# A list-scheduled hybrid block on one core: the durations in the planner's table are replaced, and a change of GpSimd's code gets a price

## The chip, the cores and the metric

The kernel runs on one core of a Trainium2 chip. The metric is the device time of one execution in microseconds (us). Five engines of the core work side by side, each through its own instructions in order: TensorE (PE, matrix products), VectorE (DVE), ScalarE (ACT), GpSimd (POOL) and SyncE (SP, which issues transfers). Semaphores order the engines among each other.

## The reference

The reference is a network of two layers on 272 tokens (16 learned ones ahead of 256) of width 1024, all in fp32. Cut to what matters:

```python
for i in range(2):
    hn = rms_norm(h, norm_mix_g[i])
    rq, rk, rv, rg, hq, hf, hi, hg, dq, dk, dv, mg = split(hn @ w_in[i])
    o_ret = rms(retention(rope(rq), rope(rk), rv)) * silu(rg)      # chunks of 128, a state
    o_hg = rms(hgrn2(hq, hf, hi)) * silu(hg)                       # gated linear recurrence
    o_da = rms(diff_attention(rope(dq), rope(dk), dv)) * subln_g   # softmax minus lam * softmax
    y = sum(sigmoid(mg) * (stack(o_ret, o_hg, o_da) @ w_branch[i]))
    h = h + y @ w_out[i]
    u = conv3(rms_norm(h, norm_ffn_g[i]) @ w_ffn_in[i])            # 3 taps along the tokens
    h = h + (silu(u_gate) * u_val) @ w_ffn_out[i]
return rms_norm(h, norm_final_g)
```

## The kernel before, in words

**The work.** The features lie on the partitions and the 272 tokens in the free dimension, so each weight tile of 128x128 is the stationary operand of a product with 272 columns (258 for some). fp32 accuracy comes from a split of both sides in a high and a low float32r part, so each weight tile gives three matmuls: `xh` by `whi` (L915), `xl` by `whi` (L916) and `xh` by `wlo` (L917), into a PSUM tile called `main`. These are the "main" matmuls; everything else that PE does is called a side matmul here.

**The weights.** SP brings in 512 KB chunks of eight tiles (`wraw`, three buffers). ACT copies a chunk to `whi`, DVE subtracts to get `wlo` (`_Weights.next`). This goes on through the whole run and is the largest part of both engines' work.

**The rest.** In each layer a normalisation gives `rstd` (squares summed, `ms` on PE by a matrix of ones, then two ACTIVATEs `rstd` on ACT after a load of ACT's function table). The first four products of a normalisation read the unscaled `h` (split into `xh`, `xl`) and are scaled behind the product; from the fifth on (`DEFER = 4`, `Norm.next`) they read `y = h * rstd`, which POOL forms in eight pieces, ACT rounds to `xh` and DVE completes to `xl`. There are four such normalisations ahead of products: two in each layer, the second one ahead of the conv FFN's input product, called fi here.

- HGRN2: a cumulative product by levels, in which PE adds shifted copies (`lev`, L1107) of what DVE has formed (`hf`, `hq`, `extra`), and then `pm`, `px`, `ho` with the values `vt` and `vm`. The values come through a path of their own: ACT copies them out of PSUM (`vsrc`), POOL takes the halves apart (`apart`), SP transposes by DMA (`turned`), POOL puts them together (`vt`), and copies the last tokens out (`tails`), which PE turns (`vm`).
- Differential attention: scores `ds`, then row sums and a combination of two softmaxes on DVE (`two_a`), turned on PE (`wt`, L1317), made to `wts` on ACT and POOL, then `do` by the values. The heads' outputs are normalised over the partitions with POOL's PARTITION_ALL_REDUCE (`hr<-hsq`).
- The convolution: three taps as ACT's `two_b` and DVE's SCALAR_TENSOR_TENSOR on `two_b`, then `ghi` and `glo`.

**What sets the order.** Nothing is issued as it is written. Every call to an engine goes through `_Engine.__getattr__`, which works out a `cost` from the method and the number `n` of elements to a partition and files an operation with `_Plan.add`, along with a due time `key`. Due times run on a clock that each main matmul triple moves on by its own cost (L905). Then `_Plan.order` walks a planned time line: on each engine it takes, among the operations whose inputs are there in the plan, the one that can start first, and among those the one with the smallest `key`. An input from another engine counts as there `CROSS` = 0.4 us behind its end; PE adds `BACK` = 0.09 us where a main follows a side matmul, a side matmul takes its turn by `key + HOLD` (3.0 us), and nothing but mains may start more than `EARLY` = 12 us ahead of its key. A weight chunk is due `LEAD` = 6 us ahead of its first use. The order found is then issued as it stands, so an error of the plan shows on the chip as an engine that waits for a row which stands too late in another engine's order.

In the planned time line an engine without work is first moved on to the time at which its next operation becomes ready, and the operation is then chosen:

```python
            if op is None:
                engines[e] = t
                continue
```

In the profile all of this is under L607, the one line in which the planned operations are called; the main matmuls, `lev`, `wt` and a few others have lines of their own.

Of the kernel before, what the change touches and what calls it, by code (L numbers as in the profile page):

```python
# [13 lines left out]
F32R = mybir.dt.float32r  # L14
# [11 lines left out]
T = META + SEQ  # L26
# [11 lines left out]
BANK = 512  # L38
# [49 lines left out]
def _ktiles(name):  # L88
    return FK if name == "fo" else KD
# [267 lines left out]
class _Plan:  # L357
# [3 lines left out]
    CROSS = 0.4  # L361
    FREE = 0.5
    SWITCH = 1.3
    SETS = {AF.Exp: "le", AF.Ln: "le", AF.Silu: "silu", AF.Sigmoid: "sigmoid"}

    def __init__(self, tc):
# [87 lines left out]
    def order(self):  # L454

        times, mains = [m.key for m in self.main], set(self.main)
        for op in self.ops:
            i = bisect.bisect_right(times, op.key - EARLY) - 1
            if i >= 0 and op not in mains:
                self.queue(op, self.main[i])  # L460
        left = {}
        for op in self.ops:
            for n in op.tiles:
                left[n] = left.get(n, 0) + 1
        free = {tag: [0.0] * k for tag, k in self.room.items()}
        held, out = set(), []
        engines = {"pe": 0.0, "act": 0.0, "dve": 0.0, "pool": 0.0, "sp": 0.0}
        later = {e: [] for e in engines}
        now = {e: [] for e in engines}
        count = 0  # L470
        tables = "le"
        beside = False

        def push(op):
            nonlocal count
            count += 1
            heapq.heappush(later[op.engine], (op.ready, count, op))

        for op in self.ops:
            if op.need == 0:  # L480
                push(op)

        def start(op, t):

            want = {}
            for n in op.tiles:
                if n not in held:
                    want[self.tag[n]] = want.get(self.tag[n], 0) + 1
            for tag, k in want.items():
# [12 lines left out]
        self.busy = {e: 0.0 for e in engines}  # L502
        todo = len(self.ops)
        while len(out) < todo:
            best = None
            for e, t0 in engines.items():
                while later[e] and later[e][0][0] <= t0:
                    _, c, op = heapq.heappop(later[e])
                    now[e].append((c, op))
                found = None  # L510
                for c, op in now[e]:
                    t = start(op, t0)
                    if t is not None and (found is None or (t, rank(op, t), c) < found[:3]):
                        found = (t, rank(op, t), c, op)
                if later[e]:
                    t1 = later[e][0][0]
                    if found is None or t1 < found[0]:
                        found = (t1, 0.0, -1, None)
                if found is not None and (best is None or found[0] < best[0]):
                    best = found + (e,)  # L520
            if best is None:
                raise RuntimeError("no order: " + str([(e, [o.tiles for _, o in now[e]][:4]) for e in now]))
            t, _, c, op, e = best
# [3 lines that stand above are left out]
            now[e].remove((c, op))  # L527
            cost = op.cost
            if op.func in self.SETS and self.SETS[op.func] != tables:
                tables = self.SETS[op.func]  # L530
                cost += self.SWITCH
                if tables == "le":
                    out.append(None)
                    todo += 1
            for n in op.tiles:
                if n not in held:
                    held.add(n)
                    f = free[self.tag[n]]
                    f.remove(min(f))
            if e == "pe":  # L540
                if op in mains:
                    cost += BACK if beside else 0.0
                beside = op not in mains
            engines[e] = t + cost
            self.busy[e] += cost
            done = t + cost + (2.0 if e == "sp" else 0.0)
            for n in op.tiles:
                left[n] -= 1
                if left[n] == 0:
                    free[self.tag[n]].append(done + self.FREE)  # L550
            for o in op.after:
                o.need -= 1
                if o.engine != e:
                    o.fed = max(o.fed, done + self.CROSS)
                o.ready = max(o.ready, done + (self.CROSS if o.engine != e else 0.0))
                if o.need == 0:
                    push(o)
            if op.run is not None:
                out.append(op)
            else:  # L560
                todo -= 1
        return out
# [11 lines left out]
class _Engine:  # L574
# [5 lines left out]
    def __getattr__(self, method):  # L580
        f = getattr(self.engine, method)

        def call(*args, **kw):
            aps = [(k, x) for k, x in list(enumerate(args)) + list(kw.items()) if isinstance(x, bass.AP)]
            outs = [x for k, x in aps if k in (0, "out", "accum_out")]
            ins = [x for k, x in aps if k not in (0, "out", "accum_out")]
            n = math.prod(outs[0].shape[1:])
            cost = self.fixed + self.each * n
            if self.name == "act":
                cost += 0.093 * (len(aps) - 2) - (0.043 if ins[0].tensor.name in self.plan.psum else 0.0)  # L590
            elif self.name == "pool" and method != "memset":
                cost += 1.6e-3 * n
            if method == "partition_all_reduce":
                cost = 0.4 + 5.4e-3 * n
            if method == "reciprocal":
                cost += 7 * self.each * n
            elif method == "tensor_tensor_scan":
                cost += self.each * n
            elif method == "transpose":
                cost = 0.11  # L600
            elif method == "matmul" and args[1].dtype == F32R:
                cost = max(0.107, n / 2400 + 0.003)
            elif method == "matmul":
                cost = max(0.214 if args[1].shape[-1] > 32 else 0.07, 4 * n / 2400)
            elif method == "dma_start":
                cost = self.fixed + self.each * n * outs[0].shape[0]
            self.plan.add(self.name, lambda: f(*args, **kw), cost, outs, ins, args[2] if method == "activation" else None)  # L607

        return call

# [55 lines left out]

def _trace(ctx, tc, plan, a, depth, probe):
    nc = tc.nc
    act = _Engine(plan, nc.scalar, "act", 0.094, 0.833e-3)
    dve = _Engine(plan, nc.vector, "dve", 0.068, 1.042e-3)  # L670
    pe = _Engine(plan, nc.tensor, "pe", 0.0, 4 / 2400)
    pool = _Engine(plan, nc.gpsimd, "pool", 0.04, 0.85e-3)
    sync = _Engine(plan, nc.sync, "sp", 0.06, 4 / 360e3)
# [218 lines left out]
    def products(xs, name, j, t0=0):  # L892
# [9 lines left out]
        if (name, j) == ("fo", 3):  # L902

            to[j, 1] = main()[:, 1, :]
        cost = 3 * ((T - t0) / 2400 + 0.003)  # L905
        left = dict.fromkeys(to, _ktiles(name))
        for _, i, k, f in tiles:
            hi, lo = (x[:, t0:] for x in xs(k))
# [80 lines left out]
    for li in range(depth):  # L989
# [4 lines left out]
        t0 = T0 if last else 0  # L994
# [389 lines left out]
        def block(name):  # L1384
            if name not in st:
                st[name] = slot4(name)
            return st[name]
# [9 lines left out]
        def final():  # L1397
# [12 lines left out]
            for t in range(2):  # L1410
                for k in range(KD):
                    pe.matmul(accs[t][k // 4][:, k % 4 * P : (k % 4 + 1) * P], h[:, k, tokens(t)], ident, is_transpose=True, start=k % 4 == 0, stop=False)
            cost = 3 * (BANK / 2400 + 0.012)
            groups = [(t, c) for t in range(2) for c in range(2)]
            chunks = {}
            order = [(k, t, c) for k in range(FK - LATE) for t, c in groups]
# [36 lines left out]
        for name, j in ORDER:  # L1453
# [18 lines left out]
            elif name[0] == "*":  # L1472
                plan.key = clock[0] - MARGIN
                n = name[1:]
                if n == "b2":
                    blocks = [st["da0"], st["da1"]]
                else:
                    t = st["rg" if n == "b0" else "hg"]
# [6 lines left out]
            if name in BASE:  # L1485
# [18 lines left out]
                elif name in ("dq", "dk"):  # L1504
                    t = block(f"{name}{j // 2}")
# [12 lines left out]
                elif name in ("hi", "dv"):  # L1518
                    n = name[0] + "v"
# [13 lines left out]
                else:  # L1533
                    t = block(f"{name}{j // 2}")
# [95 lines left out]
```

## Time and profile before

| | us |
|---|---|
| median of 3 runs | 1305.88 |
| the three runs | 1304.24, 1306.25, 1305.88 |
| profiled execution | 1305.7 |
| its span | 1303.9 |
| PE busy | 1285.8 (99%) |
| DVE busy | 986.7 (76%) |
| ACT busy | 786.7 (60%) |
| POOL busy | 270.3 (21%) |

The span is the time from the first to the last instruction; some 1.8 us of the execution's time lie around it. The mean granted clock of PE was 0.998 of full speed. A row of a timeline gives the start in us from the start of the span, the duration in us, the engine, the line, the operation, what it writes and reads, and in square brackets the idle time of that engine ahead of it with what ended it. A group of equal instructions that follow one another is one row with its count behind the x. A row of the waits gives the waiting engine's operation and the one that released it, then the sum in us, the number of times, and the longest.

### The profile page before, as it was taken

The numbers are of one execution on the slowest core, as the hardware profiler recorded it, in microseconds if no ns is written. First come the engines' busy times: TensorE is split into PE (matmuls) and PEld (weight loads), VectorE is DVE, ScalarE is ACT, GpSimd is POOL, SyncE is SP. The second block draws the span as 40 slices with busy tenths as digits, with TensorE's granted clock in tenths as the row PEclk, the third lists the DMA queues.
The fourth block names the chain that finished last, engine by engine and source line by source line (L and its number), as shares of the span: only waits on it lengthen the run. The fifth ranks groups of instructions, "written<-read, shape, count | busy, mean of one in ns | idle before, by whom it ended". The sixth has DMA issues, their size and how long they took to land.

```text
span 1303.9 us, 28637 instructions
## 1 busy us (share of the span) xinstructions
PE 1285.8 (99%) x11678; PEld 1256.7 (96%) x11678; DVE 986.7 (76%) x1589; ACT 786.7 (60%) x1282; POOL 270.3 (21%) x300
## 2 busy tenths in 40 slices
PE   9999999999999999999999999999999999999998
PEld 9999989999999999999999999899999999999986
DVE  7685897798686789886575768877986867898843
ACT  6746444746576567666456474447466765776643
POOL 5021262423422020000030212634223220200000
PEclk9999999999999999999999999999999999999999
DMA  7664665643744545555555646655446446466653
GB/s 272 200 179 147 173 178 155 164 160 125 199 138 157 182 156 178 183 173 183 175 178 185 186 149 185 179 155 168 159 138 199 145 162 198 144 207 196 201 190 112
DMA packets 86868, 225.36 MB, mean 173 GB/s; under 512 B 32976, under 2 KB 33104, under 8 KB 86736
## 3 DMA queue, kind: packets, MB, share of 16 engines
q1 hardware_dynamic: 86448, 223.00, 55.3%
q8 instruction: 92, 1.51, 0.5%
q10 hardware_dynamic: 288, 0.52, 0.1%
q14 instruction: 40, 0.33, 0.1%
HBM read 216.16 MB, written 1.05 MB: 167 GB/s over the span
## 4 chain that ended last, share of the span: by engine, by line
PE 88%; DVE 9%; issue 1%; ACT 1%; DMA 0%; SPq 0%; DVEq 0%; ACTq 0%
PE main L915 26%; PE main L917 26%; PE main L916 25%; DVE wlo L607 2%; PE fo L1430 2%; PE fo L1431 2%; PE fo L1429 2%; DVE two_b L607 1%; DVE two_a L607 1%; PE lev L1107 1%; PE ds L1291 1%; PE ho L607 1%; PE ro L607 1%; PE do L607 1%; DVE two_c L607 1%
## 5 line engine op out<-in xcount | busy, mean ns | idle before, releaser
L915 PE MATMUL main<-xh,whi 128*128 128x272 f32 (+1 forms) x2368 | 682.6, 288 | 0.8 <-ACT whi L607 0.8
L917 PE MATMUL main<-xh,wlo 128*128 128x272 f32 (+1 forms) x2368 | 673.9, 285 | 1.3 <-DVE wlo L607 0.7
L916 PE MATMUL main<-xl,whi 128*128 128x272 f32 (+1 forms) x2368 | 673.3, 284 | 1.5 <-DVE xl L607 1.5
L607 DVE TENSOR_TENSOR wlo<-wraw,whi 128x1024 fp32r<-128x1024 f32 (+1 forms) x411 | 512.0, 1250 | 187.8 <-ACT whi L607 186.6
L607 ACT ACTIVATE whi<-wraw 128x1024 fp32r<-128x1024 f32 (+1 forms) x411 | 427.5, 1042 | 250.9 <-PE main L916 166.3
L917 PEld LDWEIGHTS main<-xh,wlo 128*128 128x128 f32 x2368 | 446.5, 189 | 3.1 <-DVE wlo L607 2.3
L916 PEld LDWEIGHTS main<-xl,whi 128*128 128x128 f32 x2368 | 446.6, 189 | 2.2 <-DVE xl L607 1.9
L915 PEld LDWEIGHTS main<-xh,whi 128*128 128x128 f32 x2368 | 446.7, 189 | 2.0 <-ACT whi L607 1.0
L607 POOL TENSOR_TENSOR y<-h,rstd 128x272 f32<-128x272 f32 x32 | 34.6, 1112 | 318.1 <-ACT rstd L607 318.1
L607 POOL PARTITION_ALL_REDUCE hr<-hsq x36 | 65.8, 1837 | 88.9 <-ACT hsq L607 85.9
L607 DVE SCALAR_TENSOR_TENSOR two_b<-main,small,two_b 128x256 f32<-128x256 f32 (+2 forms) x144 | 65.3, 487 | 24.4 <-ACT two_b L607 22.7
L607 POOL COPY apart<-vsrc 128x512 uint16<-128x512 uint16 x48 | 40.7, 867 | 145.2 <-ACT vsrc L607 145.0
L607 ACT ACTIVATE two_b<-main,small 128x272 f32<-128x272 f32 (+1 forms) x72 | 37.3, 566 | 23.8 <-PE main L917 22.7
L915 PE MATMUL main<-ghi,whi 128*128 128x272 f32 x176 | 51.0, 290 | 0.0
L916 PE MATMUL main<-glo,whi 128*128 128x272 f32 x176 | 50.6, 287 | 0.0
L917 PE MATMUL main<-ghi,wlo 128*128 128x272 f32 x176 | 50.3, 286 | 0.0
L607 POOL COPY vt<-turned 128x512 uint16<-128x512 uint16 x32 | 37.0, 1160 | 29.2 <-DMA turned<-apart 29.0
L915 PE MATMUL main<-b0hi,whi 128*128 128x272 f32 (+1 forms) x128 | 37.9, 296 | 0.0
L915 PE MATMUL main<-b1hi,whi 128*128 128x272 f32 (+1 forms) x128 | 37.8, 296 | 0.0
L915 PE MATMUL main<-yhi,whi 128*128 128x272 f32 (+1 forms) x128 | 36.4, 284 | 0.0
L917 PE MATMUL main<-b0hi,wlo 128*128 128x272 f32 (+1 forms) x128 | 36.4, 284 | 0.0
L917 PE MATMUL main<-yhi,wlo 128*128 128x272 f32 (+1 forms) x128 | 36.3, 284 | 0.0
(235 smaller groups left out, 1970.1 us busy)
## 6 DMA issues: line engine op xcount, KB each, us to landing
wraw<-in_w SPq DMA_DIRECT2D x402, 512.0 KB, 3.4
h<-in_h SPq DMA_DIRECT2D x4, 272.0 KB, 5.1
dec<-in_dec SPq DMA_DIRECT2D x2, 544.0 KB, 4.9
wraw<-in_w SPq DMA_DIRECT2D x4, 256.0 KB, 4.2
const<-in_const SPq DMA_DIRECT2D x1, 937.0 KB, 5.6
turned<-apart SPq DMA_TRANSPOSE x48, 4.0
gain<-in_gl SPq DMA_DIRECT2D x1, 512.0 KB, 5.1
out<-y ACTq DMA_DIRECT2D x2, 256.0 KB, 2.8
```

What stands on the lines that cost most here:

```text
L607: self.plan.add(self.name, lambda: f(*args, **kw), cost, outs, ins, args[2] if method == "activation" else None)
L915: nc.tensor.matmul(o, wh, hi, start=first, stop=False)
L916: nc.tensor.matmul(o, wh, lo, start=False, stop=False)
L917: nc.tensor.matmul(o, wl, hi, start=False, stop=last)
L1107: nc.tensor.matmul(o, keys, x, start=True, stop=True)
L1291: nc.tensor.matmul(ss[m][:, at : at + nk], q[half, hd, q0 : q0 + P], k[half, hd, :nk], start=True, stop=True)
L1429: nc.tensor.matmul(o, gh, wh, start=False, stop=False)
L1430: nc.tensor.matmul(o, gl, wh, start=False, stop=False)
L1431: nc.tensor.matmul(o, gh, wl, start=False, stop=end)
```

## The change

Only the planner's numbers differ; the operations of the program and what they read and write are the same. `_Plan` gets `RELOAD = 8.0`: POOL's `tensor_tensor` and `partition_all_reduce` are filed with their method as their kind, and where the kind differs from the one before, the operation is set 8 us behind the time at which the planned line has POOL, which for an engine that has had no work is the time at which the operation became ready. The formula of `_Engine.__getattr__` is written anew: the fixed part of an ACT operation rises from 0.094 to 0.2 us and of a DVE operation from 0.068 to 0.145 us, POOL's operations get formulas of their own, a transposing DMA 0.7 us more, and a float32r matmul outside of the mains (`ho`, `do`, `lev` and the like) now goes by the general matmul's formula. A main triple costs 0.01 us instead of 0.003 us beyond its columns, three times: 0.370 us instead of 0.349 us for 272 columns.

```diff
+    RELOAD = 8.0
...
-        tables = "le"
+        tables, code = "le", "tensor_tensor"
...
+            if e == "pool" and op.func is not None:
+                if op.func != code:
+                    code, t = op.func, max(t, engines[e] + self.RELOAD)
             engines[e] = t + cost
...
             cost = self.fixed + self.each * n
+            kind = args[2] if method == "activation" else None
             if self.name == "act":
                 cost += 0.093 * (len(aps) - 2) - (0.043 if ins[0].tensor.name in self.plan.psum else 0.0)
-            elif self.name == "pool" and method != "memset":
-                cost += 1.6e-3 * n
-            if method == "partition_all_reduce":
-                cost = 0.4 + 5.4e-3 * n
-            if method == "reciprocal":
+            elif method == "tensor_scalar":
+                cost += 0.065 * (len(aps) - 2) - 0.14
+            elif method in ("scalar_tensor_tensor", "stream_shuffle", "tensor_tensor_reduce"):
+                cost += 0.06
+            elif method == "reciprocal":
                 cost += 7 * self.each * n
-            elif method == "tensor_tensor_scan":
-                cost += self.each * n
+            elif self.name == "pool" and method == "tensor_tensor":
+                cost, kind = 0.55 + 2.1e-3 * n, method
+            elif self.name == "pool" and method == "tensor_copy":
+                cost = 0.35 + 1.0e-3 * n
+            elif method == "partition_all_reduce":
+                cost, kind = 0.2 + 6.3e-3 * n, method
             elif method == "transpose":
                 cost = 0.11
-            elif method == "matmul" and args[1].dtype == F32R:
-                cost = max(0.107, n / 2400 + 0.003)
             elif method == "matmul":
                 cost = max(0.214 if args[1].shape[-1] > 32 else 0.07, 4 * n / 2400)
             elif method == "dma_start":
-                cost = self.fixed + self.each * n * outs[0].shape[0]
+                cost = self.fixed + self.each * n * outs[0].shape[0] + (0.7 if kw.get("transpose") else 0.0)
...
-    act = _Engine(plan, nc.scalar, "act", 0.094, 0.833e-3)
-    dve = _Engine(plan, nc.vector, "dve", 0.068, 1.042e-3)
+    act = _Engine(plan, nc.scalar, "act", 0.2, 0.833e-3)
+    dve = _Engine(plan, nc.vector, "dve", 0.145, 1.052e-3)
...
-        cost = 3 * ((T - t0) / 2400 + 0.003)
+        cost = 3 * ((T - t0) / 2400 + 0.01)
...
-            cost = 3 * (BANK / 2400 + 0.012)
+            cost = 3 * (BANK / 2400 + 0.0133)
```

All five engines' orders change. Three places show how; the lines of the changed kernel are seven higher, and the numbers of the tiles agree.

PE in the second layer's HGRN2, where the tails of the values are turned (`vm`), the keys' and queries' product `pm` is made and a level `lev` begins. Before:

```order
L917 MATMUL main_1321<-xh_14_89,wlo_1327 128x258
L607 MATMUL pm_1299<-qt_1287,kt_1286 128x128
L607 MATMUL vm_1283<-const_79,tails_1269 128x128
L915 MATMUL main_1329<-xh_16_91,whi_1331 128x258
L916 MATMUL main_1329<-xl_17_92,whi_1331 128x258
L917 MATMUL main_1329<-xh_16_91,wlo_1332 128x258
L1107 MATMUL lev_1293<-extra_1290,hf_506_1205 32x32 x32
```

And in the changed kernel:

```order
L924 MATMUL main_1321<-xh_14_89,wlo_1327 128x258
L614 MATMUL vm_1283<-const_79,tails_1269 128x128
L922 MATMUL main_1321<-xh_14_89,whi_1326 128x258
...
L614 MATMUL pm_1299<-qt_1287,kt_1286 128x128
L922 MATMUL main_1321<-xh_14_89,whi_1326 128x258
L923 MATMUL main_1321<-xl_15_90,whi_1326 128x258
L924 MATMUL main_1321<-xh_14_89,wlo_1327 128x258
L1114 MATMUL lev_1293<-extra_1290,hf_506_1205 32x32 x32
```

`vm` moved ahead of `pm`, with six mains between them, and both stand ahead of the last mains of tile 1321; counted in mains, `vm` comes 12 of them sooner.

PE in the first layer's attention, where `do` takes the last tokens' weights `tw`, which DVE forms out of `wt`. Before:

```order
L607 MATMUL wt_602<-const_79,dt_560 128x128
L915 MATMUL main_668<-xh_14_89,whi_673 128x272
L916 MATMUL main_668<-xl_15_90,whi_673 128x272
L917 MATMUL main_668<-xh_14_89,wlo_674 128x272
...
L607 MATMUL do_604<-tw_603,vs_519 128x128
```

And in the changed kernel:

```order
L614 MATMUL wt_602<-const_79,dt_560 128x128
L922 MATMUL main_676<-xh_14_89,whi_681 128x272
L923 MATMUL main_676<-xl_15_90,whi_681 128x272
L924 MATMUL main_676<-xh_14_89,wlo_682 128x272
...
L614 MATMUL do_604<-tw_603,vs_519 128x128
```

Nine mains stood between `wt` and `do` before, 18 stand there now, and the pair has moved back by some 50 rows.

ACT ahead of the first layer's fi, where `rstd` is formed. Before:

```order
L607 ACTIVATE whi_934<-wraw_933 128x1024
L569 ACT_TABLE_LOAD
L607 ACTIVATE rstd_93<-ms_911,eps_84 128x272
L607 ACTIVATE rstd_93<-rstd_93 128x272
L607 ACTIVATE whi_937<-wraw_936 128x1024
L607 ACTIVATE whi_943<-wraw_942 128x1024
L607 ACTIVATE two_b_922<-two_a_921,small_76 128x272 x2
L607 ACTIVATE xh_16_91<-y_950,small_76 128x272 x3
```

And in the changed kernel:

```order
L614 ACTIVATE whi_934<-wraw_933 128x1024
L614 ACTIVATE whi_937<-wraw_936 128x1024
L573 ACT_TABLE_LOAD
L614 ACTIVATE rstd_93<-ms_911,eps_84 128x272
L614 ACTIVATE rstd_93<-rstd_93 128x272
L614 ACTIVATE whi_943<-wraw_942 128x1024
L614 ACTIVATE two_b_922<-two_a_921,small_76 128x272 x2
L614 ACTIVATE whi_946<-wraw_945 128x1024
```

The copy `whi_937` moved ahead of the table load and of `rstd`, and the three `xh` moved behind the next weights (the first of them by eight rows).

More of the change, by code (lines that the diff above doesn't have):

```diff
@@ L605, in call @@
             elif method == "dma_start":
-                cost = self.fixed + self.each * n * outs[0].shape[0]
-            self.plan.add(self.name, lambda: f(*args, **kw), cost, outs, ins, args[2] if method == "activation" else None)
+                cost = self.fixed + self.each * n * outs[0].shape[0] + (0.7 if kw.get("transpose") else 0.0)
+            self.plan.add(self.name, lambda: f(*args, **kw), cost, outs, ins, kind)
         return call
```

## The prediction

> **What bounds the kernel now.** I read the page's busy times first.
>
> ```profile
> span 1303.9 us, 28637 instructions
> PE 1285.8 (99%) x11678; PEld 1256.7 (96%) x11678; DVE 986.7 (76%) x1589; ACT 786.7 (60%) x1282; POOL 270.3 (21%) x300
> ```
>
> PE is busy in 1285.8 of 1303.9 us. The change adds and removes no matmul, so it can reach only the 18.1 us of idle PE, and the first and last few of those belong to loads and to the final transfers. Next I read what PE waits for, from the waits:
>
> ```profile
> PE lev L1107 <- DVE hf L607: 3.2, 2, 1.7
> PE main L916 <- DVE xl L607: 1.5, 2, 1.1
> PE ho L607 <- DVE ho L607: 1.4, 2, 0.8
> PE wt L1317 <- DVE two_a L607: 1.1, 3, 0.5
> PE warm L607 <- POOL eps L607: 1.0, 1, 1.0
> PE main L915 <- ACT whi L607: 0.8, 1, 0.8
> PE main L917 <- DVE wlo L607: 0.7, 3, 0.3
> PE lev L1107 <- DVE tot L607: 0.4, 1, 0.4
> PE lev L1107 <- DVE hq L607: 0.4, 1, 0.4
> PE main L917 <- issue: 0.4, 1, 0.4
> PE do L607 <- DVE tw L607: 0.4, 1, 0.4
> PE lev L1107 <- ACT qt L607: 0.3, 1, 0.3
> PE wt L607 <- DVE wts L607: 0.2, 1, 0.2
> ```
>
> They add up to 11.8 us. The 1.0 behind `eps`, the 0.8 behind `whi` and a part of `wlo` are the program's start; 0.4 is "issue". About 9.3 us are waits for a side engine in the middle, which an order can move: this is all that can be won, 0.7% of the time, and no engine but PE can become the bound as a whole. What can be lost has no such limit: every side result that stands too late in another engine's row adds a wait.
>
> **The change part by part.** I compared the two orders, took each PE row that waits for another engine, and counted how many rows its source and it have moved. Where PE's row moved later and its source did not, the wait goes.
>
> *Attention and the second HGRN2 outputs, a gain.* The two longest of these rows:
>
> ```profile
> 265.90 0.35 PE L607 MATMUL ho<-at,vt 128*128 128x128 f32 x1 [0.81 <-DVE ho L607]
> 323.85 0.49 PE L607 MATMUL do<-tw,vs 128*128 128x128 f32 x2 [0.35 <-DVE tw L607]
> 740.07 0.28 PE L915 MATMUL main<-xh,whi 128*128 128x258 f32 x1
> 740.18 0.28 PE L916 MATMUL main<-xl,whi 128*128 128x258 f32 x1
> ```
>
> A main takes a step of 0.12 us (740.07 to 740.18). `ho` at 265.9 stands 21 mains later in the changed order and its twin of layer 1 some 24, about 2.5 us, while DVE has one `wlo` more ahead of it, 1.2 us: the 1.4 us go. `do<-tw` has nine more mains between it and the `wt` whose result it waits for, 1.1 us against 0.35 us waited, and the `wt` rows move by 9 to 60 mains with their sources ahead. Of 1.1 + 0.4 + 0.2 = 1.7 us I take 1.6. Together -3.0 us. No other work covers this: it was PE's own idle time. The branch's last values come up to 57 rows later; the branch's first product needs them at a row that did not move; PE had no wait there, and I take none.
>
> *The tails of the values, a loss.*
>
> ```profile
> 82.63 0.91 POOL L607 COPY vt<-turned 128x512 uint16<-128x512 uint16 x1 [1.43 <-DMA turned<-apart]
> 83.45 1.24 POOL L607 COPY tails<-vsrc 128x32 f32<-128x32 f32 x1
> 739.55 1.27 POOL L607 COPY tails<-vsrc 128x32 f32<-128x32 f32 x1
> 741.69 0.27 PE L607 MATMUL vm<-const,tails 128*128 128x128 f32 x1
> 741.72 0.37 PE L915 MATMUL main<-xh,whi 128*128 128x258 f32 x1
> 741.92 0.28 PE L916 MATMUL main<-xl,whi 128*128 128x258 f32 x1
> ```
>
> In layer 1 POOL ends `tails` at 739.55 + 1.27 = 740.82, and `vm` ran 0.87 us later. The changed order has `vm` 12 mains sooner, so PE is there at about 740.07 and POOL's row is where it was: 0.75 us lost. In layer 0 `vm` comes 10 mains sooner, and POOL now has `vt`, which waits for a transfer, ahead of the second half of `apart` instead of behind it, so what filled that wait comes after it: 0.3 without the swap's 0.55, 0.8 with it; I take 0.6. Sum +1.35 us, from 0.3 (should the transposes land sooner) to 2.0.
>
> *The norm ahead of fi in layer 0.* ACT's row shows what `rstd` waits for and POOL's when `y` starts:
>
> ```profile
> 471.01 1.28 ACT L569 ACT_TABLE_LOAD   x1
> 473.11 0.49 ACT L607 ACTIVATE rstd<-ms,eps 128x272 f32<-128x272 f32 x1 [0.82 <-PE ms L607]
> 473.97 1.05 ACT L607 ACTIVATE whi<-wraw 128x1024 fp32r<-128x1024 f32 x1
> 474.15 6.60 POOL L607 TENSOR_TENSOR y<-h,rstd 128x272 f32<-128x272 f32 x6 [66.64 <-ACT rstd L607]
> 479.12 3.79 DVE L607 SCALAR_TENSOR_TENSOR two_b<-two_a,small,two_b 128x271 f32<-128x271 f32 x4
> 483.47 0.48 DVE L607 SCALAR_TENSOR_TENSOR xl<-y,small,xh 128x272 fp32r<-128x272 f32 x1
> 483.88 1.21 DVE L607 TENSOR_TENSOR wlo<-wraw,whi 128x1024 fp32r<-128x1024 f32 x1
> 491.17 0.29 PE L916 MATMUL main<-xl,whi 128*128 128x272 f32 x1
> 491.32 1.73 DVE L607 SCALAR_TENSOR_TENSOR two_b<-two_a,small,two_b 128x271 f32<-128x271 f32 x4
> 494.65 0.39 PE L916 MATMUL main<-xl,whi 128*128 128x272 f32 x1 [0.35 <-DVE xl L607]
> ```
>
> [...] The plan, which starts the 8 us at readiness, takes `y` to come 8 us later than it does, and so files `xh` and `xl` late: the first `xl` stands 15 rows later on DVE. Those rows run from 483.88 to the end of the four `two_b` at 493.0, 9.1 us, less three other `xl` of 0.41 each among them, 7.9 us. So `xl` would start at 483.5 + 7.9 = 491.4 and end at 491.9, when PE wants it at 491.17: 0.7 us late. On top, the copy of 1.05 us now stands ahead of the table load of 1.28, and both behind a main just ahead of `ms`: `rstd` ends about 2.1 us later. Eight `y` then lie 2.1 us further into a stretch where DVE never rests, and beside them the four `two_b` took 0.95 us each, against 0.43 at 491.32: about 1.0 us more, so `xl` is 1.7 late. In return the old waits of this stretch, 0.35 here and about as much for two `wlo`, go. Net +0.7 us, from -0.3 (no lateness of `rstd` felt) to +1.7 (nothing given back).
>
> [...]
>
> *The norm ahead of fi in layer 1.*
>
> ```profile
> 1116.89 1.28 ACT L569 ACT_TABLE_LOAD   x1
> 1118.19 0.49 ACT L607 ACTIVATE rstd<-ms,eps 128x272 f32<-128x272 f32 x1
> 1137.25 0.39 PE L916 MATMUL main<-xl,whi 128*128 128x258 f32 x1 [1.15 <-DVE xl L607]
> ```
>
> Here the load ahead of `rstd` drops out of the changed order (31 loads become 29) and `ms` comes three mains later: `rstd` comes 1.28 - 0.37 = 0.9 us sooner, DVE is relieved by about 0.4, and the `xl` for which PE waits 1.15 us is issued ahead of one `wlo`, 1.2 us. But the first `xl`s stand 8 to 14 rows later and a `wlo` takes over part of the wait. I take -0.8, from -1.3 to +1.0.
>
> *What is left.*
>
> ```profile
> 29.16 2.39 POOL L607 TENSOR_TENSOR hq<-hq,rstd 128x544 f32<-128x544 f32 x1
> ```
>
> At the program's start `ms` comes 15 mains later and POOL's `hq` stands ahead of four `y` instead of one; PE waits for none of these `xl` before, so I take +0.2 (0 to 1.2, half of `hq`). In the second HGRN2 half of each layer PE waits for a chain on DVE (`lev` behind `hf`, 3.2 us) whose rows are the same; three mains fewer (layer 0) and three more (layer 1) stand ahead of it, 0.37 each way, 0 in sum. PE goes from mains to side matmuls 140 times instead of 132; a main behind a side matmul takes 0.37 instead of 0.28 us (741.72 against 741.92), so 8 x 0.09 = +0.7. No transfer is among PE's waits, and weights only at the start and at fi, so the new order of SP's rows costs nothing.
>
> Sum: -3.0 + 1.35 + 0.7 - 0.8 + 0.2 + 0 + 0.7 = -0.85 us, from the profiled 1305.7 to 1304.85. That execution lies 0.2 under the median of 1305.88, so I predict 1305.0.
>
> **The rivals.** About 0.2%, 2.6 us, is what a measurement of this kernel can tell from no change: below 1303.3 is faster, above 1308.5 slower.
>
> - *The truer durations hold everywhere.* The same -3.0, and at the norms all `xl` and `wlo` waits outside the start go too (1.5 + 0.6), `vm` finds its tails since the transposes land sooner; the switches remain: -3.0 - 2.1 + 0.7 = -4.4, 1301.5. For it: PE waits in these very rows. Against it: DVE is without a pause at the norms, so an order there moves waits rather than ends them.
> - *The 8 us make the norms late, slower.* The place is the first `xl`s behind `y` in both fi and at the start. If DVE stays at half speed beside `y` longer, or `xh`, which stands behind the next `whi`, holds `xl` up, each fi costs its full lateness with nothing given back: 1.7 + 0.7 (one `xl` more late) for that `xh` in layer 0, 1.7 in layer 1, and half of `hq`'s 2.39 = 1.2 at the start. That replaces my +0.7, -0.8 and +0.2 by 5.3: -0.95 + 5.3 = +4.35, 1310.2. It decides once the lateness over the three norms passes 3.5 us. For it: the first `xl` is already 0.7 late by rows alone. Against it: layer 1's `rstd` comes sooner.
> - *It does nothing:* the rows that moved are not those which PE waits for, within 0.5 us of 1305.9. Against it: `ho` and `do` are exactly such rows.
>
> [...]
>
> **How the numbers follow.** My forecast has 0.52, with a range of its own of 1302.4 to 1307.6 (the bounds of the terms: vm 1.0 down and 0.7 up, norms 1.5 down and 2.8 up, not all at once); of it 0.07 lies below 1303.3 and 0.04 above 1308.5. All-better 0.22, of it 0.20 faster; late norms 0.22, of it 0.20 slower; nothing 0.04. So faster 0.27, same 0.49, slower 0.24. The range runs from 1301.2 to 1309.6, which leaves out half of each outer rival, 2 in 10.
>
> **What would show it.** In the changed profile's PE waits, `ho <- ho`, `do <- tw` and `wt <- two_a` should be gone or under 0.8 us together; a row `vm <- POOL tails` should appear, about 1.35 us in two; `main <- xl` should show one wait of 1 to 2 us near 491 and none near 1137; `y` should still start 0.1 us behind `rstd`, which should end near 476 in layer 0. I am wrong if the waits' sum rises by over 2 us, with `xl` at the norms in front, or if `lev` waits grow: then a chain that I took for unmoved has moved.

## The result: slower by 9.5 us, and the profile after

| | before | after |
|---|---|---|
| median of 6 runs each, us | 1306.07 (1304.24 to 1307.39) | 1315.58 (1314.07 to 1316.07) |
| ratio, 95% interval | | 1.0071 (1.0058 to 1.0084) |
| profiled execution / its span, us | 1305.7 / 1303.9 | 1314.07 / 1312.3 |

The changed kernel is slower by more than the range of the prediction allowed. Its busy times have hardly moved:

```profile
span 1312.3 us, 28618 instructions
PE 1286.3 (98%) x11678; PEld 1257.5 (96%) x11678; DVE 982.7 (75%) x1589; ACT 784.0 (60%) x1280; POOL 277.0 (21%) x300
```

PE is busy for 0.5 us more, in a span longer by 8.4. So the loss is idle time of PE, and the waits name it (the sum, the number of times, the longest):

```profile
PE vm L614 <- POOL tails L614: 6.3, 3, 2.6
PE lev L1114 <- DVE hf L614: 4.6, 3, 2.2
PE main L924 <- DVE wlo L614: 2.9, 5, 1.5
PE main L923 <- DVE xl L614: 2.9, 4, 1.2
PE warm L614 <- POOL eps L614: 1.0, 1, 1.0
PE main L923 <- issue: 0.5, 1, 0.5
PE lev L1114 <- ACT extra L614: 0.5, 1, 0.5
PE main L922 <- ACT whi L614: 0.5, 1, 0.5
PE ho L614 <- DVE ho L614: 0.4, 1, 0.4
PE wt L614 <- DVE wts L614: 0.4, 1, 0.4
```

They add up to 20.0 us against 11.8, 8.2 more. One row that the profile of before lacks altogether makes 6.3 of it. Its three waits are these, PE's rows in its timeline:

```profile
260.52 0.33 PE L614 MATMUL vm<-const,tails 128*128 128x128 f32 x1 [1.25 <-POOL tails L614]
348.29 0.33 PE L614 MATMUL vm<-const,tails 128*128 128x128 f32 x1 [2.59 <-POOL tails L614]
1002.61 0.33 PE L614 MATMUL vm<-const,tails 128*128 128x128 f32 x1 [2.43 <-POOL tails L614]
```

All three are in the attention's values (`dv`), none in HGRN2. Before, PE came to the same three products without a wait, but with little to spare:

```profile
258.89 0.27 PE L607 MATMUL vm<-const,tails 128*128 128x128 f32 x1
344.91 0.27 PE L607 MATMUL vm<-const,tails 128*128 128x128 f32 x1
994.59 0.27 PE L607 MATMUL vm<-const,tails 128*128 128x128 f32 x1
```

Their `tails` ended on POOL at 258.27, 344.22 and 993.47, that is 0.62, 0.69 and 1.12 us ahead. What POOL does ahead of the longest of the three waits stands in its own timeline. Before:

```profile
332.84 1.17 POOL L607 COPY apart<-vsrc 128x512 uint16<-128x512 uint16 x2 [0.76 <-ACT vsrc L607]
333.96 1.35 POOL L607 COPY tails<-vsrc 128x32 f32<-128x32 f32 x2
337.24 1.91 POOL L607 COPY vt<-turned 128x512 uint16<-128x512 uint16 x1 [1.93 <-DMA turned<-apart]
339.06 1.65 POOL L607 COPY apart<-vsrc 128x512 uint16<-128x512 uint16 x1
340.66 1.76 POOL L607 COPY vt<-turned 128x512 uint16<-128x512 uint16 x1
342.34 1.58 POOL L607 COPY apart<-vsrc 128x512 uint16<-128x512 uint16 x1
343.86 0.36 POOL L607 COPY tails<-vsrc 128x32 f32<-128x32 f32 x2
```

After:

```profile
333.47 1.63 POOL L614 COPY apart<-vsrc 128x512 uint16<-128x512 uint16 x2 [0.92 <-ACT vsrc L614]
335.08 1.06 POOL L614 PARTITION_ALL_REDUCE hr<-hsq  x1
336.02 1.02 POOL L614 COPY tails<-vsrc 128x32 f32<-128x32 f32 x2
339.88 0.79 POOL L614 COPY vt<-turned 128x512 uint16<-128x512 uint16 x1 [2.84 <-DMA turned<-apart]
340.58 2.44 POOL L614 COPY da<-tw 128x64 f32<-128x64 f32 x2
342.96 1.83 POOL L614 COPY vt<-turned 128x512 uint16<-128x512 uint16 x1
344.71 3.22 POOL L614 COPY apart<-vsrc 128x512 uint16<-128x512 uint16 x2
347.88 0.36 POOL L614 COPY tails<-vsrc 128x32 f32<-128x32 f32 x2
```

The last two of the `tails` that `vm` needs stand at the end of both. From the first `apart` to their end it takes 343.86 + 0.36 - 332.84 = 11.38 us before and 14.77 after, 3.4 more. The attention's last all-reduce (1.06) and its two `da` copies (2.44), which before stood ahead of the row's start, are in it now and take 3.3 us with their overlaps; the wait for the transposes is 0.9 longer, and the copies proper take 0.8 less. In layer 1 the stretch ahead of 1002.61 is 13.84 us against 10.84, with an all-reduce inside it that stood ahead of it before; its two `da` copies are inside in both, and it waits 0.2 us for transposes against 2.4 before. Near 260 no attention row is inside; the stretch is 12.15 us against 11.56 and starts 1.6 us later, and two `apart` and two `vt` of 1.6 to 1.8 us each stand ahead of the last `tails`. So what the three have in common is the place of the `tails` behind other rows of POOL; a longer wait for a transfer is part of one of them only.

How the time runs apart, from the starts of the same main matmul in both traces: after is 1.4 us behind at 40 us, 0.4 at 330, 5.3 at 360, 5.3 at 955, 8.8 at 1030 and 8.4 at the end. So two short stretches, each around a late `vm`, make 4.9 and 3.5 of the 8.4 us. Of the 1.4 of the program's start 1.0 is won back by 330, the wait at 260 included.

### The profile page after: what moved, and what is told of

It reads as the page before. It is cut to its first block, busy times and chain, and to the rows that moved or that the text cites. A ratio compares the mean times of both kernels' runs of the same rounds, so it can differ in the third digit from the quotient of the medians.

```text
span 1312.3 us, 28618 instructions
## 1 busy us (share of the span) xinstructions
PE 1286.3 (98%) x11678; PEld 1257.5 (96%) x11678; DVE 982.7 (75%) x1589; ACT 784.0 (60%) x1280; POOL 277.0 (21%) x300
## 4 chain that ended last, share of the span: by engine, by line
PE 84%; DVE 8%; POOL 2%; DMA 2%; issue 2%; ACT 1%; SPq 0%; DVEq 0%; ACTq 0%; POOLq 0%
PE main L922 25%; PE main L923 24%; PE main L924 24%; DVE wlo L614 3%; PE fo L1436 2%; PE fo L1437 2%; PE fo L1438 2%; PE lev L1114 1%; PE ds L1298 1%; DMA wraw<-in_w 1%; PE ro L614 1%; DVE two_c L614 1%; DVE two_b L614 1%; DMA turned<-apart 1%; PE do L614 1%
## 5 line engine op out<-in xcount | busy, mean ns | idle before, releaser
L614 POOL PARTITION_ALL_REDUCE hr<-hsq x36 | 75.3, 2110 | 120.7 <-ACT hsq L614 120.6
L614 POOL COPY apart<-vsrc 128x512 uint16<-128x512 uint16 x48 | 45.1, 955 | 145.0 <-ACT vsrc L614 145.0
```

## The experiments

The theory at the start was that the loss is PE's wait at `vm` for rows that the new order lets stand late on POOL; the rivals were the 8 us of `RELOAD`, the new fixed costs of ACT and DVE as such, and POOL's new formulas. Times are medians; each ratio is against the kernel before, measured beside it on the same chip (1305.2 to 1305.7).

**Which number of the change is it?** `RELOAD` put to nothing in the changed kernel:

```diff
-    RELOAD = 8.0
+    RELOAD = 0.0
```

> The changed kernel with RELOAD = 0 instead of 8.0, all other numbers as changed. Theory A (the loss is POOL's queue: the attention's late all-reduces and copies stand among the next half's value copies, so the tails come late and PE waits at vm, 6.3 us in three waits, plus about 1.5 us at half clock behind one of them): POOL's order in those places is the same as in the changed kernel, so the vm waits stay at 5 to 7 us; only the xl waits (2.9 us) shrink by 1 to 2; the time is 1313 to 1315. Theory B (the 8 us make the norms and all that follows late): the time falls to 1308 or less. Theory C (my prediction's sum, with the tails worth 1.35): cannot be told apart from B here.

Measured: 1314.1 us, ratio 1.0068 (1.0053 to 1.0083), `vm` waits 4.5 us. That is 8.9 us over before on its chip, against 9.5 for the changed kernel: the loss is there without the 8 us. The converse, the kernel before with only the 8 us:

> The kernel before with RELOAD = 8.0 alone; all durations in the plan as before. POOL's order at the attention's ends is that of the kernel before. Theory A: no vm wait; the only loss is late xl and wlo at the two fi norms and HGRN2's first outputs, 0 to 3 us: 1305 to 1308. My slower rival (the 8 us make the norms late) had 5.3 us for it, which would give 1310 or more; theory B (RELOAD is the cause) 1313 or more.

Measured: 1307.35 us, 1.0011 (1.0002 to 1.0021), with one `vm` wait of 1.0 us, where none was expected, and 3.3 us for `xl`. So the 8 us cost some 1.6 us by themselves. Next, the changed kernel with the old fixed costs of ACT and DVE:

```diff
-    act = _Engine(plan, nc.scalar, "act", 0.2, 0.833e-3)
-    dve = _Engine(plan, nc.vector, "dve", 0.145, 1.052e-3)
+    act = _Engine(plan, nc.scalar, "act", 0.094, 0.833e-3)
+    dve = _Engine(plan, nc.vector, "dve", 0.068, 1.042e-3)
```

> The changed kernel with the old fixed costs of ACT (0.094) and DVE (0.068 and 1.042e-3), RELOAD and all else as changed. Theory A: POOL's order at the attention's ends is that of the kernel before again (all-reduces and da ahead of the value copies), so vm waits under 1 us and the time falls to about 1307, with the xl waits at the norms left (2 to 3 us). Theory B: RELOAD is still there, so the time stays at 1313 or more.

Measured: 1310.88 us, 1.0045 (1.003 to 1.006): six tenths of the loss stay, 3.1 us at `vm` in four waits, none over 0.9, and 3.1 at `wt` that the changed kernel had been rid of. Neither theory had this: A expected about 1307, B 1313 or more. The kernel before with only these two lines new:

> The kernel before with the new fixed costs of ACT and DVE alone; no RELOAD, old costs of POOL, side and main matmuls. Theory A: the all-reduces of the attention's ends stand among the value copies here too, so PE waits at vm for 4 to 8 us and the time is 1311 to 1316. Theory B: without RELOAD the time is that of the kernel before, 1304 to 1307.

Measured: 1311.22 us, 1.0051 (1.0035 to 1.0068), with one `vm` wait of 2.3 us, where theory A expected 4 to 8, and 4.9 us for `wlo` and 2.9 for `xl`. These costs alone therefore bring six tenths of the loss, and one of the waits at `vm`. The last, POOL's old formulas back in the changed kernel:

> The changed kernel with the old cost formulas of POOL's operations (tensor_tensor, copies, all-reduce), RELOAD and the new ACT, DVE and main costs kept. POOL's order has the first half's last all-reduces and da among the value copies as in the changed kernel. Theory A: vm waits of 3 to 7 us remain and the time is 1311 to 1315, since it is the later attention chain on ACT and DVE that brings the all-reduces there. Rival E (POOL's own new costs make it choose a bad order): vm waits under 1.5 us and a time of 1308 or less.

Measured: 1309.92 us, 1.0035 (1.0023 to 1.0047), `vm` 2.8 us in two, between the two expectations. None of these three parts carries the loss alone; each of them undone leaves over four tenths of it. The new costs of the main triples and the side matmuls and the 0.7 us of a transposing DMA were not undone on their own, so their shares stay open. The cause is sought in the order, then.

**Is it the wait at `vm`?** The tails' copies of HGRN2 and the attention go from POOL to ACT, which has made their source (both lines; the retention's tails stay on POOL):

```diff
-                    pool.tensor_copy(tails[:, 0], src[:, :, 2 * P :])
+                    act.activation(tails[:, 0], src[:, :, 2 * P :], AF.Copy)
```

> The changed kernel, with the copies of the values' last tokens (tails, 128x32) in HGRN2 and attention done by ACT instead of POOL; the plan's numbers as changed. Theory A: the vm waits go, since the tails no longer stand in POOL's queue, and the time falls by 5 to 8 us to 1308 to 1311. If the waits for tails only moved on to the next consumer of POOL's values (do and ho waiting for vt), the time stays above 1313 and those waits appear. Theory B: no difference over 1 us.

Measured: 1305.67 us in 10 runs, 1.0005 (0.9996 to 1.0015); PE's waits have no `vm` left:

```profile
PE lev L1114 <- DVE hf L614: 4.6, 3, 2.2
PE main L923 <- DVE xl L614: 3.2, 3, 1.2
...
```

The loss is gone although `lev`, `xl` and the start are as they were or worse, and the time lies below the 1308 to 1311 that was expected. The trace's span is 9.0 us shorter than the changed kernel's (1303.3 against 1312.3): 6.3 are the `vm` waits, 1.1 the other waits in sum (20.0 us come down to 12.6), and the rest is about what the changed kernel lost at half clock behind one of its waits (1.5 us, see the last section). The control, the same edit on the kernel before, where there is no such wait to win:

> The kernel before with the tails copied by ACT instead of POOL; a control for the run with the same edit in the changed kernel. Theory A: the kernel before has no vm wait, so the edit removes none; the time is that of the kernel before within 2 us, and the 9 to 10 us that the edit gave in the changed kernel are its vm waits. If the edit helps by itself (ACT is a better place for these copies whatever the order), the time falls by several us, below 1302.

Measured: 1305.57 us, 1.0 (0.9991 to 1.0009). So the edit brings nothing of its own. With it, the 8 us and the ACT and DVE costs were taken out once more:

> The changed kernel with the tails on ACT and RELOAD = 0: a candidate to beat both kernels. No vm waits, and the xl waits at the two fi norms (about 1.2 each) smaller: 1303 to 1305.5 if the start does not get worse; 1305.5 to 1307 if it does (the start varied by 1.4 to 4 us among the runs with these costs).

Measured: 1304.57 us in 10 runs, 0.9995 (0.9985 to 1.0004), the lowest median of all but not to be told from before.

> The run with the old fixed costs of ACT and DVE (1310.9, vm waits 3.1 us in four), with the tails on ACT: theory A2 says that the vm waits of 3.1 us go and the time falls to about 1308; its other waits (wt 3.1, lev 5.8) have nothing to do with tails and stay. If the time falls below 1305, more than vm was lost to POOL's queue there.

Measured: 1309.48 us, 1.0031 (1.0018 to 1.0044): `wt` 3.2 us and `lev` some 6 stay, as expected, but the time fell by 1.4 us only (from 1310.88), about half of what waited at `vm`, and 0.6 of that stays at the `vm` of the retention. With the tails out of the way, the new costs of ACT and DVE are worth 3.6 us: 4.0 over before without them (1309.48 against 1305.44), 0.4 with them (1305.67 against 1305.22).

**Is it the attention's late rows ahead of the tails?** An edge in the plan holds the first half's last all-reduce, and so the `da` behind it, until the second half's tails are done:

```diff
+            if b == 0:
+                st["held"] = [x for x in plan.ops[n0:] if x.engine == "pool"][0]
...
+                plan.queue(st["held"], st["freed"])
```

> The changed kernel with one more edge in the plan for each layer: the last all-reduce of the first attention half (and so the da copies behind it) starts on POOL only after the second half's tails have been copied. Nothing else is set. Theory A (those all-reduces and copies stand in POOL's queue ahead of the tails): the vm waits of 2.6 and 2.4 us near 348 and 1002 go, the one of 1.3 near 260 (where no attention work stands) stays, so vm waits are 1 to 2 us in sum, the half-clock stretch behind 348 goes too, and the time falls by 5 to 7 us to about 1309. The attention's results are not needed until some 70 us later, so nothing new waits for them. Rival D (POOL's value copies themselves are slow or late, by DVE beside them or late transposes): the waits shrink by less than a third and the time stays above 1313.

Measured: 1316.56 us, 1.0081 (1.0066 to 1.0096), no better than the changed kernel. The `vm` waits are 4.2 us instead of 6.3 (1.3, 2.0 and 0.9), but other rows of PE wait longer, `b2hi` and `b2lo` of the attention among them (1.7 us). A miss of the theory in that form. POOL's timeline:

```profile
336.54 0.36 POOL L614 COPY tails<-vsrc 128x32 f32<-128x32 f32 x2
341.51 0.79 POOL L614 COPY vt<-turned 128x512 uint16<-128x512 uint16 x1 [4.61 <-DMA turned<-apart]
...
347.07 1.35 POOL L614 COPY tails<-vsrc 128x32 f32<-128x32 f32 x2
```

The foreign rows are gone, as the edge asks, and `tails` ends at 348.42, where it ended in the changed kernel (348.24). POOL now idles 4.61 us for the transposes instead, for `vt` still stands ahead. The all-reduce had filled a hole that was there anyway. The row starts 1.5 us later in this run, so from the first `apart` to the end it is 13.4 us against 14.8: these rows are a part of the lateness, not all of it. Next, `vt` filed 6 us later (`plan.key += 6.0` around its copies), alone and with the edge:

> The changed kernel with the second copies of the value path (vt, which wait for the transposing transfers) filed 6 us later, so that in POOL's row the next half's apart and tails stand ahead of most of them; nothing else set. Theory A2 (after the last runs: the tails are late because of all that stands ahead of them in POOL's queue, of which the attention's copies are one part and the vt that wait for transposes the other): near 260 no vt is ahead of the tails and the wait of 1.3 goes; near 1002 two vt (2.6 us and 1.3 idle) go and with them the 2.4; near 348 one of two vt goes (1.8) and under 1 us is left. vm waits under 1.5 us in sum, time 1308 to 1311, unless the later vt make ho, do or px wait (then up to 2 us of that is lost again). Rival D (the copies are slow or late by themselves): vm waits stay above 4 us.

Measured: 1312.81 us, 1.0056 (1.004 to 1.0072). The wait at 1002 went, where no `vt` stood ahead of the last tails any more (7.8 us from the first `apart` to their end, 13.84 before that); the one at 348 stayed, 2.2 us, where one `vt` and the `da` still did. The `vm` waits sum to 3.5 us, under 1.5 expected: 0.7 are left near 260, and the `vm` of the retention now waits 0.6.

> The two last edits together: the first attention half's last all-reduce and da, and the vt, behind the tails. Theory A2: nothing but one vt is ahead of any tails that the copies do not need; vm waits are 0.5 us or less in sum. The time is below that of the vt edit alone by the rest of the wait near 348, less what the attention's late end costs at b2 in layer 1 (0.9 + 0.8 us in the run with that edit alone): 1308 to 1311.

Measured: 1317.92 us, 1.0097 (1.0074 to 1.0121). A miss again: a later due time does not bind, and the plan put a `vt` ahead of the tails in both places; POOL idles 4.66 and 4.76 us for its transfer, and the `vm` waits are 5.8 us in four.

**Place in the row, or POOL's speed?** Taking the copies to ACT had taken away the row and POOL's speed at once (`apart` takes 0.6 us a copy in some stretches and 1.6 in others). So the copies stay on POOL, and one edge puts the attention's `tails` ahead of one of the two `apart`, and with it ahead of every `vt`:

```diff
+                    n0 = len(plan.ops)
                     src = values(ps, st[f"{n}t{b}"], (j % 2) * 2 * P)
...
+                    if name in ("dv",):
+                        plan.queue([x for x in plan.ops[n0:] if x.engine == "pool"][0], plan.ops[-1])
```

> The changed kernel, with one more rule for the planner: in the attention's values, one of the two `apart` copies of each half waits for that half's `tails`, so that in POOL's row every `tails` stands ahead of every `vt`; the copies stay on POOL and keep their durations. Theory A (PE's wait comes from the place in POOL's row: `tails` stand behind `vt`, which wait for the transposing transfers, and behind late attention work): the `vm` waits of 6.3 us fall under 1 us although the transposes land as late as before, and the time falls by 5 to 8 us to about 1308, as with the copies on ACT (1305.67). Theory B (POOL is too slow beside DVE, 1.6 us for an `apart` copy instead of 0.6, whatever the row): at least half of the `vm` waits stay, over 3 us, and the time is over 1311. Theory C (the wait moves on to whoever reads `vt`, now behind the tails): no `vm` wait but a new PE wait of 3 us or more behind `vt` or `da`, and the time stays over 1311.

Measured: 1307.47 us in 11 runs, 1.0011 (1.0003 to 1.002). PE's waits have no row of `vm`, and no new one behind `vt` or `da`:

```profile
PE lev L1114 <- DVE hf L614: 3.6, 2, 2.2
PE main L924 <- DVE wlo L614: 3.5, 7, 1.1
PE main L923 <- DVE xl L614: 3.4, 3, 1.3
...
```

POOL's row at the same place:

```profile
333.83 0.80 POOL L614 COPY apart<-vsrc 128x512 uint16<-128x512 uint16 x1 [1.57 <-ACT vsrc L614]
334.61 1.06 POOL L614 PARTITION_ALL_REDUCE hr<-hsq  x1
335.54 0.87 POOL L614 COPY tails<-vsrc 128x32 f32<-128x32 f32 x2
336.36 0.61 POOL L614 COPY apart<-vsrc 128x512 uint16<-128x512 uint16 x1
337.17 0.42 POOL L614 COPY da<-tw 128x64 f32<-128x64 f32 x2 [0.20 <-DVE tw L614]
339.72 0.62 POOL L614 COPY apart<-vsrc 128x512 uint16<-128x512 uint16 x1 [2.13 <-ACT vsrc L614]
340.28 0.36 POOL L614 COPY tails<-vsrc 128x32 f32<-128x32 f32 x2
340.58 0.62 POOL L614 COPY apart<-vsrc 128x512 uint16<-128x512 uint16 x1
341.14 3.50 POOL L614 COPY vt<-turned 128x512 uint16<-128x512 uint16 x2
```

The all-reduce and the `da` stand there still. But nothing ahead of the tails waits for a transfer, and they end at 340.64, 7.6 us sooner. Where the row of the changed kernel waits 2.84 us for `turned`, this one waits only for its source, `vsrc`. PE even comes 24 mains sooner to this `vm`, 12 near 260 and 21 in layer 1, and finds its tails each time. The place in the row decides, not the engine. The copies are also faster here (0.6 us for an `apart` against 1.6), so their pace came with the place. Near 260 it did not: the copies ahead of the tails' end are as slow as in the changed kernel (`apart` 1.58 us, two `tails` 2.42), and there is no wait either, with 0.05 us to spare. The runs do not part the two further. Against the changed kernel the gain is 8.1 us between the medians.

Without the 8 us as well, and the control on the kernel before:

> As the run with every `tails` of the attention ahead of `vt`, and the plan's 8 us for GpSimd's change of code set to 0. Theory A: no `vm` waits of note either, and the time within 2 us of that run; with the copies on ACT instead, the same step was worth 1.1 us (1305.67 to 1304.57), which is inside both intervals. If the 8 us had a part in the loss after all, it would now show alone: over 3 us faster than that run.

Measured: 1306.46 us in 11 runs, 1.0006 (0.9997 to 1.0014). That is 1.0 us below the run with the 8 us, inside both intervals.

> The kernel before with the same rule for the `tails`, as a control: it has 0 us of `vm` waits to lose, so all theories expect it within 1 us of before, 1305.5. If it is over 3 us faster, then the rule brings something of its own, and the run of the changed kernel with it would say less on the cause.

Measured: 1307.04 us in 11 runs, 1.001 (1.0001 to 1.0019), so the edge by itself costs a microsecond or so, a little more than the 1 us allowed for, rather than brings one. No version was found that is measurably faster than before.

## Why the prediction was wrong, and where it was right

**The step that failed** is the term of the tails, +1.35 us, with its premise that "POOL's row is where it was". It prices the `vm` of HGRN2 alone. The four `vm` of the attention, which take `tails` by the same path, stood at nothing without a reason: I listed only rows of PE that wait before, and these did not. Three of them had a slack of 0.62, 0.69 and 1.12 us. In the changed kernel PE comes to the first and the third six mains sooner (0.7 us) and to the second at the same place, while POOL's row from the first `apart` to the tails' end is longer by 0.6, 3.4 and 3.0 us. In place of 1.35 us the runs showed waits of 6.3 at `vm`, and with the tails out of that place, on ACT or ahead of `vt`, none.

"The branch's last values come up to 57 rows later ... PE had no wait there, and I take none" held for the row that it names: the changed kernel has no wait for `b2hi` or `b2lo`. What it left out is the queue on the way. I followed the values on PE and not on POOL, where the attention's late all-reduce, and near 348 its `da` copies, moved into the stretch in which POOL forms the next values. They are a part of the lateness: held back alone, they left 4.2 us of `vm` waits.

**The place was wrong.** I placed those 1.35 us in HGRN2. There is no wait there in the changed kernel, in either layer. POOL's and PE's rows of layer 1:

```profile
741.19 0.77 POOL L614 COPY vt<-turned 128x512 uint16<-128x512 uint16 x1
742.90 1.27 POOL L614 COPY tails<-vsrc 128x32 f32<-128x32 f32 x1
744.80 0.27 PE L614 MATMUL vm<-const,tails 128*128 128x128 f32 x1
```

PE came to `vm` where I had put it (744.80, less the 4.76 us by which the trace runs late there, is 740.04 against 740.07). But `vt` no longer waits 1.13 us for its transposes, so `tails` ends at 744.17, ahead of PE. That was the lower end of my bounds, "should the transposes land sooner"; I had held the transfers fixed. In layer 0 `vm` comes 9 mains sooner (612 ahead of it against 621), not 10, and does not wait either.

**SP's rows.** "No transfer is among PE's waits ... so the new order of SP's rows costs nothing" reads the waits one step deep. A transfer was among POOL's waits, and PE waits for POOL. It counted for one of the three waits. SP's queue ahead of 348, before:

```profile
333.49 1.22 SPq L607 DMA_TRANSPOSE turned<-apart  x1
335.12 0.33 SPq L607 DMA_DIRECT2D wraw<-in_w  x1
335.50 1.19 SPq L607 DMA_TRANSPOSE turned<-apart  x1
```

And after:

```profile
334.57 2.59 SPq L614 DMA_TRANSPOSE turned<-apart  x2
337.26 4.78 SPq L614 DMA_DIRECT2D wraw<-in_w  x3
```

From the first issue to the first `vt` it is 3.75 us before (to 337.24) and 5.31 after (to 339.88). Whether the later landing comes from the two transposes back to back or from the weights around them was not tried, and stays open.

**The smaller terms.** `ho`, `do` and `wt` went nearly as predicted: of 1.4 + 0.4 + 1.1 + 0.2 us, 0.8 is left (0.4 for `ho`, 0.4 for `wt`), so 2.3 went where I took 3.0. The norm ahead of fi in layer 0 was priced at +0.7 and cost 0.4, with one `xl` wait of 0.95 us at 496.90; in layer 1 I took -0.8, and it was +0.3: the `xl` wait of 1.15 us, which was to go, stands there with 1.17. The start, +0.2, was +1.4, by waits for `wlo` (0.9) and `xl` (0.7); in the other runs with the new ACT and DVE costs it was between 0.6 and 3.8 at 40 us, and in those with the old ones between 0.3 ahead of before and 1.1 behind it. `lev`, taken as a chain that did not move, waits 1.4 us more for `hf`, 0.8 more with all its sources.

`y` starts as soon as `rstd` lets it, in layer 0 at 480.93 behind the second `rstd` row's end at 480.83, and before at 474.15 behind 474.06 (473.63 + 0.43). Neither start shows the 8 us of the plan; POOL had been idle for 60.72 and 66.64 us ahead of them, and what such a start takes without that was not shown.

What the prediction calls half speed of DVE beside `y` are these rows of before: `y` starts on POOL at 479.78, 480.71 and 481.64 and `two_b` on DVE at 480.05, 480.97 and 481.90. Each goes on by 0.93 us, in turn with the other; why was not shown.

**The rivals.** Slower it was, but not by the rival's mechanism: the norms cost 0.7 us together, and `RELOAD`, with the other numbers as changed, 1.5 us by medians (1314.1 against 1315.58), or 0.6 with each counted from before on its own chip, which is inside the intervals. The waits' sum rose by 8.2 us, over the 2 named as a sign of being wrong, but with `vm` in front and not `xl`. "The truer durations hold everywhere" fell: with the tails taken care of the kernel comes back to before, not below it.

## What to carry to other kernels

When an order changes, follow each late value through every in-order queue that it passes, also the queues of engines that are a fifth busy: a short copy for which the bound engine waits does not belong behind longer rows that nobody waits for yet, least of all behind one that waits for a transfer. Here a binding edge put it ahead where a later due time did not. And truer costs in a planner move work also into gaps that had kept another chain on time. So look at rows of the bound engine that do not wait, too, and at their slack: three of those with 0.6 to 1.1 us came to wait here. Slack alone does not tell which, for the attention's fourth `vm` had 0.2 us before and did not wait.

## What the runs showed of the hardware

In the changed kernel more was lost at one wait of PE than its length. The window behind the 2.59 us wait at 348.29, with the busy time and the instructions of PE, its weight loads, DVE, ACT and POOL, and then the granted clock (0.52):

```profile
349.60:353.00 3.40, 3.40 (x18) 3.40 (x17) 1.11 (x1) 1.06 (x1) 0.77 (x1) 0.52 0.78 236
```

For some 3.4 us, from 1.4 us behind that wait's end, PE ran at half clock, 14 mains at 0.227 us a step instead of 0.123, 1.5 us more. Before has such a stretch too, at 834, behind `lev` waits of 1.7 and 0.4 us (its window 834.00:837.00 has a granted clock of 0.50), so it is no part of the difference between the two. From 20 us to the last 20 us, these are the only such stretches in the traces of before and after. The waits of 2.19 us for `lev` at 838.49 and of 2.43 us at 1002.61 in the changed kernel had none behind them, though both are longer than the 1.7 before, so the length of the wait alone does not tell. The run with the tails ahead of `vt`, where PE's longest wait at `lev` was 2.2 us, had a mean granted clock of 0.999, against 0.997 for the changed kernel and 0.998 for before.
